# A two-layer decoder trunk on one core: FoX queries and keys by halves, w_out in landing order, memory norm emitted earlier

## The chip, the core and the metric

The kernel runs on one NeuronCore of one Trainium2 chip. The metric is the device time of one execution in microseconds, and the runs are compared by their median. The engines are TensorE (PE, matrix products; PEld is its weight load), VectorE (DVE), ScalarE (ACT), GpSimd (POOL) and SyncE (SP), which here issues all DMAs. Each engine works through its own queue in order, and semaphores hold an instruction until its data are there.

## The reference

Two identical layers on x of 256 tokens by 1024 features, in float32. Each layer does four things, all before an RMSNorm and added to x:

```python
x = x + 0.5 * swiglu(rms_norm(x, ffn1_norm[l]), ...)
x = x + hybrid_mixer(rms_norm(x, mix_norm[l]), w_in[l], ..., w_out[l])
x = x + memory_cross_attention(rms_norm(x, cross_norm[l]), rms_norm(mem, mem_norm[l]), ...)
x = x + 0.5 * swiglu(rms_norm(x, ffn2_norm[l]), ...)
```

The change is in the mixer. One projection `z = h @ w_in` gives HGRN2's q, f, i, g (four heads of 128) and FoX's q, k, v and a forget logit (eight heads of 64). HGRN2 is a gated scan over the tokens, with an output norm and gate. FoX is causal softmax attention whose scores carry the accumulated log forget gates as a bias. Their outputs are joined and multiplied by `w_out`. The cross attention reads 256 memory tokens; its keys are made from the normalized memory.

## The kernel before

**Products.** Every float32 factor is cut into a rounded high part and the rest, and a product is three matmuls, high x high, high x low and low x high (`mm3`, L379; the low x low part is left out). Weights come by DMA as 1 MB loads into three `raw` buffers (`fetch`, L126). ScalarE casts the high part (L149) and VectorE subtracts it (L150); both go into pools of seven buffers, `whi` and `wlo`, of `SLOT` columns. `plan` lists every load of the program in order, `take` (L156) hands out the next one, splits one load ahead and fetches two more beyond that.

There are three kinds of product. `xstat` (L388) has the tokens stationary and up to 512 weight columns moving: the result has tokens on the partitions. `wstat` (L420) has a 128x128 block of weights stationary and 256 tokens moving: the result is feature-major; it took two loads, 512 columns wide, and ran through all eight row blocks of a column block before the next. `rows_to_residual` (L470) contracts over the rows of w_out or another output matrix: the first two blocks for all four accumulators, then for each accumulator the last six (`TAIL`), so that the first half of the tokens is done early and its norm can start.

**Order.** The emission order is worked out at build time by a small planner (`drive`, L341). Tasks are Python generators that yield the TensorE time that they used, a latency, or an `Event`; a spawned task runs as soon as the planner's clock has reached it, before the main line. The clock is that of the plan and not the chip's: constants such as `LAT_M` say how long a task is to leave its results alone. A scheduler then places the emitted instructions on the engines' queues, with the buffers of each pool handed out as they come free. One pool, `s4`, has 19 buffers of 4 KB a partition for nearly all activations.

**The mixer** (L794). `xstat_first` makes v and the output gate. Then come, main line first: `wstat` for the forget gates `fg` and the keys `kk`; `wstat` for q; the spawn of `hgrn` (L572), which runs seven levels of a blocked scan, each with small matmuls (`al`, L589) and VectorE updates of `qf` and `kk` (L610, L612); the spawn of `memory_task` (L874), which loads and normalizes the memory, waits `LAT_M`, and transposes it to `mf`; a 260-wide `xstat` with FoX's v for heads 4 to 7 and the forget logits; the spawn of `fox_gates` (L676); `wstat` for FoX q, then k, 512 wide; a 260-wide `xstat` for the rest of v. Then two FoX lanes are spawned (`fox_lane`, L741), each with two pairs of heads one after the other: a pair's score operands are stacked (`fox_stack`, L719), scores, softmax, transposes and the product with v follow. The main line meanwhile makes the cross keys `kc` from `mf` (L858 to L865) and then contracts `w_out`, whose first four row blocks are HGRN2's (`ev_h`) and whose last four are FoX's pairs 0 to 3 (`ev_p`).

The lanes and the order before:

```python
fox_lane((lane, lane + 2), fq, fk, fv, L_, R_, oT, cmask, oh, ev_g, ev_p)
```

Of the kernel before, what the change touches and what calls it, by code (L numbers as in the profile page):

```python
# [12 lines left out]
AF = mybir.ActivationFunctionType  # L13
# [7 lines left out]
D = 1024  # L21
# [4 lines left out]
EPS = 1e-6  # L26
NEG = -1.0e30
FCH = [(c, min(512, DFF - c)) for c in range(0, DFF, 512)]
SLOT = 1040
N_S4, N_W = 19, 7  # L30
TAIL = 6
HP = 100
# [1 line left out]
LAT_NORM, LAT_X = 5.5, 6.5  # L34
LAT_LVL, LAT_AX, LAT_HN = 3.0, 1.0, 3.5
LAT_FS, LAT_FT, LAT_CQ, LAT_CS, LAT_CT = 6.0, 2.5, 2.6, 5.6, 3.0
LAT_Q, LAT_G1, LAT_G2, LAT_M = 5.0, 9.0, 2.0, 18.0
LAT_HT = 2.4
LAT_FK = 5.0

# [5 lines left out]
def hymba_kernel(  # L46
# [43 lines left out]
    def add_cols(w, l, c0, cw):  # L90
        for k0 in range(0, KT, 4):
            plan.append((kview(w, l, c0, cw, k0, 4), 4, cw))

    def add_rows(w, l, nkt):
        for k0 in range(0, nkt, 2):
            plan.append((kview(w, l, 0, D, k0, 2), 2, D))
# [7 lines left out]
    for l in range(DEPTH):  # L104
        add_ffn(ffn1_g, ffn1_u, ffn1_d, l)
        for o in (OFF_I, OFF_G, OFF_F, OFF_Q):
            add_cols(w_in, l, o, 512)
        add_cols(w_in, l, OFF_FV + 260, 260)
        add_cols(w_in, l, OFF_FQ, 512)
        add_cols(w_in, l, OFF_FK, 512)  # L110
        add_cols(w_in, l, OFF_FV, 260)
        add_cols(c_wk, l, 0, 512)
        add_cols(c_wk, l, 512, 512)
        add_rows(w_out, l, KT)
        for w in (c_wv, c_wq):
            for c0 in (0, 512):
                add_cols(w, l, c0, 512)
        add_rows(c_wo, l, KT)
        add_ffn(ffn2_g, ffn2_u, ffn2_d, l)
# [16 lines left out]
    def split(i):  # L136
        while len(pieces) <= min(i, len(plan) - 1):
            j = len(pieces)
            fetch(j + LA_D - 1)
            _, nk, cw = plan[j]  # L140
            r = raws[j]
            n = max(1, SLOT // cw)
            res = []
            for k0 in range(0, nk, n):
                kk = min(n, nk - k0)
                sl = r[:, k0 * cw:(k0 + kk) * cw]
                hi = wp.tile([P, SLOT], F32R, name=nm("whi"), tag="whi")
                lo = wp.tile([P, SLOT], F32R, name=nm("wlo"), tag="wlo")
                nc.scalar.copy(out=hi[:, :kk * cw], in_=sl)  # L149
                nc.vector.tensor_tensor(out=lo[:, :kk * cw], in0=sl,  # L150
                                        in1=hi[:, :kk * cw].bitcast(F32), op=ALU.subtract)
                for k in range(kk):
                    res.append((hi[:, k * cw:(k + 1) * cw], lo[:, k * cw:(k + 1) * cw]))
            pieces.append(res)
# [264 lines left out]

    def wstat(f, use, cw=512):  # L420

        pc = take() + take()
        for b in range(cw // 256):
            ps = acc()
            for j in range(2):
                c = (2 * b + j) * P
                for kt in range(KT):
                    mm3(ps[:, j * S:(j + 1) * S], pc[kt][0][:, c:c + P], pc[kt][1][:, c:c + P],
                        f.hi(kt), f.lo(kt), kt == 0, kt == KT - 1)
                    yield T256  # L430
            use(b, ps)
# [306 lines left out]
            nc.gpsimd.tensor_copy(out=ks[oth, 1, sub, :], in_=R_[oth])  # L738
        return qs, ks

    def fox_lane(pairs, fq, fk, fv, L_, R_, oT, cmask, oh, ready, done):  # L741
        yield ready
        for pr in pairs:
            qs, ks = fox_stack(pr, fq, fk, L_, R_, oh)
            yield (LAT_FK,)
            prs = []
            for sub in range(2):
                ps = smp("fs")
                for t, o, n in SEGS:
                    for j in range(2):  # L750
                        nc.tensor.matmul(ps[:, o:o + n], lhsT=qs[:, j, sub, t * P:(t + 1) * P], rhs=ks[:, j, sub, 0:n],
                                         start=j == 0, stop=j == 1)
                yield 0.44
                pr_ = pp()
                prs.append(pr_)
                mx = small(2, "fmx")
                for t, o, n in SEGS:
                    nc.vector.tensor_tensor_reduce(out=pr_[:, o:o + n], in0=ps[:, o:o + n], in1=cmask[:, S - n:S],
                                                   scale=1.0, scalar=-3.0e38, op0=ALU.add, op1=ALU.max,
                                                   accum_out=mx[:, t:t + 1])  # L760
                nmx = small(2, "fnm")
                nc.vector.tensor_scalar(out=nmx, in0=mx, scalar1=-1.0, scalar2=None, op0=ALU.mult)
                softmax(pr_, nmx, 1.0, [(t, pr_[:, o:o + n], pr_[:, o:o + n]) for t, o, n in SEGS])
            yield (LAT_FS,)
            pTs = []
            for sub in range(2):
                pt = smp("fpt")
                for j in range(3):
                    nc.tensor.transpose(pt[:, j * P:(j + 1) * P], prs[sub][:, j * P:(j + 1) * P], ident)
                yield 3 * T1  # L770
                pT = sm.tile([P, 512], F32, name=nm("ppT"), tag="ppT", bufs=4)
                nc.scalar.copy(out=pT[:, 0:3 * P], in_=pt[:, 0:3 * P])
                pTs.append(pT)
            yield (LAT_FT,)
            pv = smp("fpv")
            for sub in range(2):
                h = 2 * pr + sub
                b0 = sub * 64
                vs = slice(h * 64, (h + 1) * 64)
                pT = pTs[sub]  # L780
                o = pv[b0:b0 + 64]
                nc.tensor.matmul(o[:, 0:P], lhsT=fv[:, 0, vs], rhs=pT[:, 0:P], start=True, stop=True)
                nc.tensor.matmul(o[:, P:S], lhsT=fv[:, 0, vs], rhs=pT[:, P:2 * P], start=True, stop=False)
                nc.tensor.matmul(o[:, P:S], lhsT=fv[:, 1, vs], rhs=pT[:, 2 * P:3 * P], start=False, stop=True)
                yield 0.64
            put_split(oT.h[1][:, pr, :], oT.l[1][:, pr, :], pv[:, 0:S])
            done[pr].fire(1.6)

    def feat_major(f, func, scale, dst):
        def use(b, ps):  # L790
            nc.scalar.activation(dst[:, 2 * b:2 * b + 2, :], ps.rearrange("p (k t) -> p k t", k=2), func, scale=scale)
        return wstat(f, use)

    def mixer(cur, l, consts, nxt_w):  # L794
        masks, tri, cmask, sel, oh = consts
# [13 lines left out]
        for t in range(NT):  # L809
            nc.scalar.activation(gw[:, t, :], pg[t], AF.Silu)  # L810
            gv = gw[:, t, :].rearrange("p (h e) -> p h e", h=4)
            nc.vector.tensor_tensor(out=gv, in0=gv, in1=onw.unsqueeze(1).to_broadcast([P, 4, P]), op=ALU.mult)

        fg = s4([P, 4, S], F32, "fg")
        kk = s4([P, 4, S], F32, "kk")
# [12 lines left out]
        q = s4([P, 4, S], F32, "hq")  # L828
        yield from feat_major(f, AF.Silu, 1.0, q)
        oT = Feat("oT")  # L830
        ev_h, ev_q, ev_m, ev_g = Event(), Event(), Event(), Event()
        ev_q.fire(LAT_Q)
        spawn(hgrn(q, fg, kk, v, gw, oT, masks, ev_q, ev_h))
        mf = Feat("mf")
        spawn(memory_task(l, wmem, mf, ev_m))
        fv = s4([P, NT, 512], F32, "fv")
        zb = small(16, "zb", bufs=2).rearrange("p (t h) -> p t h", t=NT)
        ps = []
        yield from xstat(f, 260, ps)
        for t in range(NT):  # L840
            nc.vector.tensor_tensor(out=zb[:, t, :], in0=ps[t][:, 252:260], in1=fb, op=ALU.add)
            nc.scalar.copy(out=fv[:, t, 260:512], in_=ps[t][:, 0:252])
        L_ = sm.tile([P, S], F32, name=nm("L"), tag="L", bufs=1)
        R_ = sm.tile([P, S], F32, name=nm("R"), tag="R", bufs=1)
        spawn(fox_gates(zb, L_, R_, tri, sel, ev_g))
        fq = s4([P, 4, S], F32, "fq")
        yield from feat_major(f, AF.Copy, 0.125, fq)
        fk = s4([P, 4, S], F32, "fk")
        yield from feat_major(f, AF.Copy, 1.0, fk)
        ps = []  # L850
        yield from xstat(f, 260, ps)
        for t in range(NT):
            nc.scalar.copy(out=fv[:, t, 0:260], in_=ps[t][:, 0:260])
        oT.alloc(1)
        ev_p = [Event() for _ in range(4)]
        for lane in range(2):
            spawn(fox_lane((lane, lane + 2), fq, fk, fv, L_, R_, oT, cmask, oh, ev_g, ev_p))
        kc = [[s4([P, 4, S], F32R, "kc") for _ in range(2)] for _ in range(2)]  # L858
        yield ev_m
        for c in range(2):  # L860
# [3 lines left out]

            yield from wstat(mf, use)  # L865
        nxt = Next(nxt_w, lat=LAT_X)

        def act(kt, t):
            return oT.hi(kt, t), oT.lo(kt, t)

        yield from rows_to_residual(act, KT, 1.0, TAIL, nxt, lambda kt: ev_h if kt < 4 else ev_p[kt - 4])
        return nxt, kc, mf

    def memory_task(l, wn, mf, ev):  # L874
        mf.alloc(0)
        mf.alloc(1)
        ms = []
        for t in range(NT):
            mt = s4([P, D], F32, "mem")
# [8 lines left out]
            apply_norm(mt, rs)  # L888
            ms.append(mt)
        yield (LAT_M,)  # L890
        for t in range(NT):
            for b in range(2):
                to_feat(ms[t], t, mf, b)
# [124 lines left out]
```

## Time and profile before

| | us |
|---|---|
| median of 3 runs | 1253.11 (1252.86 to 1255.58) |
| profiled execution | 1254.4 |
| its span, first to last instruction | 1252.6 |
| mean granted TensorE clock | 0.997 of full |

A row of busy time by stage gives the length of the stretch, the busy microseconds of each engine with its number of instructions, the granted clock, the share of the DMA engines and the bytes moved. A row of waits gives the engine and line that stood, what ended it, the total, how often, and the longest. A row of a group of instructions gives line, engine, operation, output and inputs, shapes and count, then busy us and mean ns, then the engine's idle time before them. Matmuls are pipelined: the next starts before the modelled end of the one before.

### The profile page before, as it was taken

What the parts mean: (1) busy time and instruction counts of PE and PEld (TensorE: products, weight loads), DVE (VectorE), ACT (ScalarE), POOL (GpSimd) and SP (SyncE); (2) the same over time, 40 slices, a digit from 0 to 9 for tenths busy, and PEclk for the clock granted to TensorE, in tenths of its full rate; (3) what the DMA queues carried; (4) which work ended last, traced back from release to release, by engine and by line L of the source; (5) the groups of instructions that cost most, each with busy time, mean ns of one, the idle gap of its engine ahead of it and who ended that gap; (6) DMA issues with size and microseconds to landing.
All of it is one profiled execution on the core that took longest, in us unless ns stands there. A gap on an engine that the chain in (4) does not pass through costs nothing.

```text
span 1252.6 us, 21298 instructions
## 1 busy us (share of the span) xinstructions
PE 1225.4 (98%) x8969; PEld 1118.6 (89%) x8969; DVE 758.6 (61%) x1108; ACT 628.4 (50%) x935; POOL 38.2 (3%) x52
## 2 busy tenths in 40 slices
PE   6999999999999999999999999999999999999997
PEld 4999988989889889998889998889998898999986
DVE  6654646597875674555474555476786766545643
ACT  5544434567854464454354454265585645534531
POOL 0000000002000000000000000000020000000000
PEclk9999999999999999999999999999999999999999
DMA  7654754654444264556474556465443633555650
GB/s 268 221 195 136 249 195 151 212 158 157 146 172 170 101 233 154 203 174 219 145 240 147 202 180 219 140 219 186 138 156 113 234 119 136 170 200 168 236 169 34
DMA packets 100752, 221.26 MB, mean 177 GB/s; under 512 B 4136, under 2 KB 16688, under 8 KB 100656
## 3 DMA queue, kind: packets, MB, share of 16 engines
q1 hardware_dynamic: 100656, 219.90, 51.6%
q8 instruction: 70, 1.15, 0.4%
q14 instruction: 26, 0.21, 0.1%
HBM read 218.84 MB, written 1.05 MB: 176 GB/s over the span
## 4 chain that ended last, share of the span: by engine, by line
PE 90%; ACT 4%; DVE 3%; DMA 1%; issue 1%; POOL 0%; SPq 0%; POOLq 0%; DVEq 0%; ACTq 0%
PE acc L380 28%; PE acc L381 28%; PE acc L382 28%; PE pt L301 1%; ACT whi L149 1%; DVE wlo L150 1%; ACT pp L713 1%; ACT fqs L729 1%; DMA mem<-in_mem_dram 1%; PE al L589 1%; DMA raw<-in_ffn_w_gate_dram 1%; ACT fks L731 1%; ACT fks L730 0%; POOL mrs L282 0%; PE cpo L381 0%
## 5 line engine op out<-in xcount | busy, mean ns | idle before, releaser
L150 DVE TENSOR_TENSOR wlo<-raw,whi 128x1024 fp32r<-128x1024 f32 x400 | 479.3, 1224 | 323.6 <-ACT whi L149 322.2
L149 ACT CAST whi<-raw 128x1024 fp32r<-128x1024 f32 x400 | 406.4, 1047 | 337.1 <-PE acc L382 183.9
L380 PE MATMUL acc<-xfh,whi 128*128 128x256 f32 x1536 | 434.9, 283 | 0.0
L381 PE MATMUL acc<-xfl,whi 128*128 128x256 f32 x1536 | 431.9, 281 | 0.0
L382 PE MATMUL acc<-xfh,wlo 128*128 128x256 f32 x1536 | 430.0, 280 | 1.9 <-DVE wlo L150 1.9
L382 PEld LDWEIGHTS acc<-xfh,wlo 128*128 128x128 f32 x1536 | 290.4, 189 | 2.2 <-DVE wlo L150 2.2
L381 PEld LDWEIGHTS acc<-xfl,whi 128*128 128x128 f32 x1536 | 290.9, 189 | 0.4
L380 PEld LDWEIGHTS acc<-xfh,whi 128*128 128x128 f32 x1536 | 289.2, 188 | 0.9
L380 PE MATMUL acc<-whi,hth 128*128 128x512 f32 x352 | 138.6, 394 | 0.0
L381 PE MATMUL acc<-wlo,hth 128*128 128x512 f32 x352 | 138.5, 393 | 0.0
L382 PE MATMUL acc<-whi,htl 128*128 128x512 f32 x352 | 138.1, 392 | 0.0
L380 PE MATMUL acc<-whi,xfh 128*128 128x512 f32 (+1 forms) x256 | 95.2, 373 | 1.8 <-ACT xfh L307 1.8
L381 PE MATMUL acc<-wlo,xfh 128*128 128x512 f32 (+1 forms) x256 | 94.5, 369 | 0.0
L382 PE MATMUL acc<-whi,xfl 128*128 128x512 f32 (+1 forms) x256 | 94.2, 368 | 0.0
L382 PEld LDWEIGHTS acc<-whi,htl 128*128 128x128 f32 x352 | 66.2, 188 | 15.1
L380 PEld LDWEIGHTS acc<-whi,hth 128*128 128x128 f32 x352 | 66.1, 188 | 14.9
L381 PEld LDWEIGHTS acc<-wlo,hth 128*128 128x128 f32 x352 | 66.1, 188 | 14.7
L380 PEld LDWEIGHTS acc<-whi,xfh 128*128 128x128 f32 x256 | 48.6, 190 | 10.3 <-ACT xfh L307 2.2
L382 PEld LDWEIGHTS acc<-whi,xfl 128*128 128x128 f32 x256 | 48.6, 190 | 8.9 <-DVE xfl L308 0.6
L288 ACT ACTIVATE jk<-xs 128x512 f32<-128x512 f32 x36 | 21.7, 603 | 68.4 <-DVE xs L482 66.6
L381 PEld LDWEIGHTS acc<-wlo,xfh 128*128 128x128 f32 x256 | 48.7, 190 | 7.9
L307 ACT CAST hth<-sil 128x512 fp32r<-128x512 f32 x36 | 22.3, 621 | 62.2 <-DVE sil L556 62.2
(228 smaller groups left out, 1340.3 us busy)
## 6 DMA issues: line engine op xcount, KB each, us to landing
raw<-in_ffn_w_down_dram SPq DMA_DIRECT2D x44, 1024.0 KB, 4.9
raw<-in_ffn_w_up_dram SPq DMA_DIRECT2D x40, 1024.0 KB, 5.3
raw<-in_ffn_w_gate_dram SPq DMA_DIRECT2D x38, 1024.0 KB, 5.2
raw<-in_w_in_dram SPq DMA_DIRECT2D x24, 1024.0 KB, 5.3
raw<-in_cross_wk_dram SPq DMA_DIRECT2D x8, 1024.0 KB, 5.1
raw<-in_w_out_dram SPq DMA_DIRECT2D x8, 1024.0 KB, 5.0
raw<-in_cross_wv_dram SPq DMA_DIRECT2D x8, 1024.0 KB, 5.2
raw<-in_cross_wq_dram SPq DMA_DIRECT2D x8, 1024.0 KB, 5.6
```

The source lines that it names most:

```text
L149: nc.scalar.copy(out=hi[:, :kk * cw], in_=sl)
L150: nc.vector.tensor_tensor(out=lo[:, :kk * cw], in0=sl, in1=hi[:, :kk * cw].bitcast(F32), op=ALU.subtract)
L288: nc.scalar.activation(dst, half(src, j), AF.Square, scale=1.0 / 32.0, accum_out=ss[:, j:j + 1])
L301: nc.tensor.transpose(pt[:, j * P:(j + 1) * P], hn[:, kt * P:(kt + 1) * P], ident)
L307: nc.scalar.copy(out=hi, in_=src)
L380: nc.tensor.matmul(ps, lhsT=lh, rhs=rh, start=start, stop=False)
L381: nc.tensor.matmul(ps, lhsT=lh, rhs=rl, start=False, stop=False)
L382: nc.tensor.matmul(ps, lhsT=ll, rhs=rh, start=False, stop=stop)
L589: nc.tensor.matmul(ps[s0:s0 + hb, c0:c0 + hb], lhsT=k[:, h, a:a + hb], rhs=rhs[:, h, a + step:a + step + hb], start=True, stop=True)
L713: nc.scalar.activation(dst, src, AF.Exp, bias=nmx[:, t:t + 1], scale=scale, accum_out=sms[:, t:t + 1])
L729: nc.scalar.copy(out=qs[own, :, sub, :], in_=qv.unsqueeze(1).to_broadcast([64, 2, S]))
L731: nc.scalar.copy(out=ks[oth, 0, sub, :], in_=kv)
```

## The change

FoX's q and k are loaded and computed by halves of 256 columns: first the halves of heads 4 to 7 (q, then k), then those of heads 0 to 3. One load holds all eight row blocks of a half, so `wstat` takes one load where it has eight blocks. The two lanes are spawned after the first two halves and run pairs 2 and 3 first, then 0 and 1; a lane's stack follows an event for its half of k, its product with v one for its half of v. The v columns are cut 264 and 256 instead of 260 and 260, and `SLOT` grows by 16 columns. `w_out` is loaded and contracted with the row blocks of pairs 2 and 3 ahead of those of 0 and 1. `memory_task` is spawned ahead of the forget gates; its feature buffers are taken after its delay, and the delay is 34 instead of 18. FoX's output buffers are taken when the first pair is done. The number of casts in a split is rounded down to a power of two.

```diff
-SLOT = 1040
+SLOT = 1056
-LAT_Q, LAT_G1, LAT_G2, LAT_M = 5.0, 9.0, 2.0, 18.0
+LAT_Q, LAT_G1, LAT_G2, LAT_M = 5.0, 9.0, 2.0, 34.0
+    def add_half(w, l, c0):
+        plan.append((kview(w, l, c0, 256, 0, KT), KT, 256))
-        add_cols(w_in, l, OFF_FV + 260, 260)
-        add_cols(w_in, l, OFF_FQ, 512)
-        add_cols(w_in, l, OFF_FK, 512)
-        add_cols(w_in, l, OFF_FV, 260)
+        add_cols(w_in, l, OFF_FV + 256, 264)
+        for c0 in (256, 0):
+            add_half(w_in, l, OFF_FQ + c0)
+            add_half(w_in, l, OFF_FK + c0)
+        add_cols(w_in, l, OFF_FV, 256)
...
-        add_rows(w_out, l, KT)
+        for k0 in (0, 2, 6, 4):
+            plan.append((kview(w_out, l, 0, D, k0, 2), 2, D))
...
-            n = max(1, SLOT // cw)
+            n = 1 << (SLOT // cw).bit_length() - 1
...
     def wstat(f, use, cw=512):
-        pc = take() + take()
+        pc = take()
+        if len(pc) < KT:
+            pc = pc + take()
...
-    def fox_lane(pairs, fq, fk, fv, L_, R_, oT, cmask, oh, ready, done):
+    def fox_lane(pairs, fq, fk, fv, L_, R_, oT, cmask, oh, ready, ev_k, ev_v, done):
         yield ready
         for pr in pairs:
+            yield ev_k[pr // 2]
             qs, ks = fox_stack(pr, fq, fk, L_, R_, oh)
...
             yield (LAT_FT,)
+            yield ev_v[pr // 2]
             pv = smp("fpv")
...
+            if 1 not in oT.h:
+                oT.alloc(1)
...
-    def feat_major(f, func, scale, dst):
+    def feat_major(f, func, scale, dst, b0=0, cw=512):
         def use(b, ps):
+            b += b0
...
-        return wstat(f, use)
+        return wstat(f, use, cw)
...
     def mixer(cur, l, consts, nxt_w):
...
+        ev_h, ev_q, ev_m, ev_g = Event(), Event(), Event(), Event()
+        mf = Feat("mf")
+        spawn(memory_task(l, wmem, mf, ev_m))
         fg = s4([P, 4, S], F32, "fg")
...
-        mf = Feat("mf")
-        spawn(memory_task(l, wmem, mf, ev_m))
...
-        yield from feat_major(f, AF.Copy, 0.125, fq)
         fk = s4([P, 4, S], F32, "fk")
-        yield from feat_major(f, AF.Copy, 1.0, fk)
+        ev_k, ev_v = [Event(), Event()], [Event(), Event()]
+        ev_p = [Event() for _ in range(4)]
+        ev_v[1].fire()
+        for hf in (1, 0):
+            yield from feat_major(f, AF.Copy, 0.125, fq, hf, 256)
+            yield from feat_major(f, AF.Copy, 1.0, fk, hf, 256)
+            ev_k[hf].fire()
+            if hf == 1:
+                for lane in range(2):
+                    spawn(fox_lane((lane + 2, lane), fq, fk, fv, L_, R_, oT, cmask, oh, ev_g, ev_k, ev_v, ev_p))
         ps = []
-        yield from xstat(f, 260, ps)
+        yield from xstat(f, 256, ps)
...
-        oT.alloc(1)
-        ev_p = [Event() for _ in range(4)]
-        for lane in range(2):
-            spawn(fox_lane((lane, lane + 2), fq, fk, fv, L_, R_, oT, cmask, oh, ev_g, ev_p))
+        ev_v[0].fire()
...
+        order = (0, 1, 2, 3, 6, 7, 4, 5)
         def act(kt, t):
+            kt = order[kt]
             return oT.hi(kt, t), oT.lo(kt, t)
...
-        yield from rows_to_residual(act, KT, 1.0, TAIL, nxt, lambda kt: ev_h if kt < 4 else ev_p[kt - 4])
+        def need(kt):
+            kt = order[kt]
+            return ev_h if kt < 4 else ev_p[kt - 4]
+
+        yield from rows_to_residual(act, KT, 1.0, TAIL, nxt, need)
...
     def memory_task(l, wn, mf, ev):
-        mf.alloc(0)
-        mf.alloc(1)
         ms = []
...
         yield (LAT_M,)
+        mf.alloc(0)
+        mf.alloc(1)
```

More of the change, by code (lines that the diff above doesn't have):

```diff
@@ L830, in mixer @@
         oT = Feat("oT")
-        ev_h, ev_q, ev_m, ev_g = Event(), Event(), Event(), Event()
         ev_q.fire(LAT_Q)
         spawn(hgrn(q, fg, kk, v, gw, oT, masks, ev_q, ev_h))
-        mf = Feat("mf")
-        spawn(memory_task(l, wmem, mf, ev_m))
         fv = s4([P, NT, 512], F32, "fv")
@@ L838, in mixer @@
         ps = []
-        yield from xstat(f, 260, ps)
+        yield from xstat(f, 264, ps)
         for t in range(NT):
-            nc.vector.tensor_tensor(out=zb[:, t, :], in0=ps[t][:, 252:260], in1=fb, op=ALU.add)
-            nc.scalar.copy(out=fv[:, t, 260:512], in_=ps[t][:, 0:252])
+            nc.vector.tensor_tensor(out=zb[:, t, :], in0=ps[t][:, 256:264], in1=fb, op=ALU.add)
+            nc.scalar.copy(out=fv[:, t, 256:512], in_=ps[t][:, 0:256])
         L_ = sm.tile([P, S], F32, name=nm("L"), tag="L", bufs=1)
@@ L846, in mixer @@
         fq = s4([P, 4, S], F32, "fq")
-        yield from feat_major(f, AF.Copy, 0.125, fq)
         fk = s4([P, 4, S], F32, "fk")
-        yield from feat_major(f, AF.Copy, 1.0, fk)
+        ev_k, ev_v = [Event(), Event()], [Event(), Event()]
[8 more added lines that the diff above has]
+                    spawn(fox_lane((lane + 2, lane), fq, fk, fv, L_, R_, oT, cmask, oh, ev_g, ev_k, ev_v, ev_p))
         ps = []
-        yield from xstat(f, 260, ps)
+        yield from xstat(f, 256, ps)
         for t in range(NT):
-            nc.scalar.copy(out=fv[:, t, 0:260], in_=ps[t][:, 0:260])
-        oT.alloc(1)
-        ev_p = [Event() for _ in range(4)]
-        for lane in range(2):
-            spawn(fox_lane((lane, lane + 2), fq, fk, fv, L_, R_, oT, cmask, oh, ev_g, ev_p))
+            nc.scalar.copy(out=fv[:, t, 0:256], in_=ps[t][:, 0:256])
+        ev_v[0].fire()
         kc = [[s4([P, 4, S], F32R, "kc") for _ in range(2)] for _ in range(2)]
```

## The prediction

> **What bounds the kernel now.** I read the page first, then who TensorE waited for in the mixer of each layer, then busy time and granted clock by stage.
>
> ```profile
> PE 1225.4 (98%) x8969; PEld 1118.6 (89%) x8969; DVE 758.6 (61%) x1108; ACT 628.4 (50%) x935; POOL 38.2 (3%) x52
> ```
>
> TensorE is busy for 98% of the span and the others for 61% at most, so only time in which TensorE stands, or runs at a lower clock, can be won. Its waits from 250 to 346 us (layer 0) and from 860 to 962 us (layer 1), columns: total us, times, longest:
>
> ```profile
> PE acc L380 <- DVE kc L308: 1.4, 1, 1.4
> PE acc L382 <- DVE wlo L150: 1.0, 1, 1.0
> PE al L589 <- DVE kk L612: 0.6, 1, 0.6
> PE al L589 <- DVE qf L580: 0.4, 1, 0.4
> PE fpv L782 <- ACT ppT L772: 0.4, 1, 0.4
> PE fs L751 <- DVE fks L734: 0.3, 2, 0.2
> ...
> PE acc L380 <- DVE kc L308: 1.5, 1, 1.5
> PE acc L382 <- DVE wlo L150: 1.0, 1, 1.0
> PE al L589 <- DVE kk L612: 0.6, 1, 0.6
> PE fpv L782 <- ACT ppT L772: 0.4, 1, 0.4
> PE fs L751 <- DVE fks L734: 0.3, 2, 0.2
> ```
>
> That is 4.1 us in 7 waits and 3.8 us in 6. Two groups: at the start of the HGRN2 scan (al, wlo: 2.0 and 1.6 us) and in the FoX rounds and behind them (fs, fpv, kc: 2.1 and 2.2 us). Nearly all end on VectorE. Next, layer 0 by stage (v and gate projection; forget gates; q; the 260-wide product with the start of the scan; FoX q, k and rest of v; cross keys with FoX; start of w_out), then two stretches of layer 1, and the costliest matmul group:
>
> ```profile
> 205.00:228.00 23.00, 22.99 (x105) 18.52 (x104) 18.23 (x21) 13.69 (x19) 2.37 (x2) 1.00 0.83 273
> 228.00:240.00 12.00, 12.00 (x102) 11.91 (x101) 5.25 (x10) 6.73 (x9) 0.00 (x0) 1.00 0.19 50
> 240.00:252.00 12.00, 12.00 (x104) 12.00 (x103) 6.49 (x10) 6.94 (x10) 0.00 (x0) 1.00 0.93 330
> 252.00:262.00 10.00, 8.99 (x190) 8.49 (x188) 8.87 (x20) 7.72 (x15) 2.39 (x2) 1.00 0.56 184
> 262.00:303.00 41.00, 40.00 (x592) 38.60 (x593) 33.20 (x58) 23.64 (x51) 5.05 (x8) 1.00 0.47 156
> 303.00:337.00 34.00, 32.91 (x270) 31.24 (x268) 30.07 (x101) 30.35 (x75) 2.01 (x3) 1.00 0.26 94
> ...
> 875.00:880.00 5.00, 3.66 (x76) 3.27 (x77) 4.45 (x6) 1.02 (x1) 0.00 (x0) 0.73 0.39 99
> 880.00:885.00 5.00, 5.00 (x97) 4.68 (x95) 3.47 (x11) 2.31 (x4) 0.00 (x0) 0.93 0.41 119
> ```
>
> ```profile
> L382 PE MATMUL acc<-xfh,wlo 128*128 128x256 f32 x1536 | 430.0, 280 | 1.9 <-DVE wlo L150 1.9
> ```
>
> Columns of the stages: length, busy us of PE, PEld, DVE, ACT, POOL, granted clock, DMA share, GB/s. Two things besides the waits are lost. A wait is counted from the modelled end of a matmul, 280 ns after its start, but in the q stage 104 matmuls start in 12.00 us, one per 0.12 us; so each of the 13 waits costs 0.16 us more, 2.1 us together. And in layer 1 the waits at the scan's start are followed by a granted clock of 0.73 and 0.93 over 5 us each: 5 x 0.27 + 5 x 0.07 = 1.7 us. Layer 0, with the same waits, kept 1.00. **Everything that the mixer's waits cost is 7.9 + 2.1 + 1.7 = 11.7 us**, the ceiling of this change.
>
> The Trainium skill, "TensorE: Matmul & The Clock Gate", section "HAM oscillation — how this bites in real kernels", gives as the rule that no idle gap of TensorE may exceed about 3.4 us. The waits above are 1.5 us at most and the clock fell all the same, so the trace does not agree that shorter gaps are free. By the rule the drop has another cause and may stay; the sum below would then be 1.7 us less of a gain, 1247.1.
>
> **The change part by part.** *Memory norm earlier.* Its instructions, both layers together (min/median/max ns):
>
> ```profile
> L288 ACT ACTIVATE mj<-mem x8: 580/587/602, 250.7 to 868.1; 128x512 f32<-128x512 f32 x8
> L288 ACT ACTIVATION_READ_ACCUMULATOR mj<-mem x8: 186/187/189, 251.2 to 868.6; 128x1 f32 x8
> L291 DVE TENSOR_TENSOR mem<-mem,wn x8: 682/686/693, 251.5 to 869.5; 128x512 f32<-128x512 f32 x8
> L295 DVE TENSOR_SCALAR mem<-mem,mrs x8: 478/484/486, 255.3 to 872.2; 128x512 f32<-128x512 f32 x8
> L880 SPq DMA_DIRECT2D mem<-in_mem_dram x4: 444/484/618, 241.7 to 856.1; - x4
> ...
>   DVE mem L295: 1.8, 4
> ```
>
> Per layer this is 4 x 0.686 + 4 x 0.484 = 4.7 us of VectorE plus 0.9 us in which its queue stands for the power on GpSimd (the last row), and 4 x 0.77 = 3.1 us of ScalarE. It sits at 251 to 260 us, in the stage where VectorE is busy 8.87 of 10 us and TensorE first stands. TensorE's lateness there is 2.0 us; taking 5.6 us out of VectorE's queue covers it, and with it the clock drop. The work goes to the forget-gate stage, busy 5.25 (VectorE) and 6.73 (ScalarE) of 12 us, where 5.6 and 3.1 fit. Its two DMAs (0.48 us of SP each) are now issued ahead of the second 264-wide load instead of ahead of the first FoX key load; that leaves a stage with a DMA share of 0.93 for one with 0.19. If ScalarE reaches the squares before memory has landed, the gate sigmoids and later weight casts queue behind them; the cover is the slack of these stages, which show no wait of TensorE. Without that cover it costs the 3.1 us of squares per layer. I take 0. Late next would be the memory transposes, wanted only by the cross keys at 303 us; they move little, since their delay grows from 18 to 34 planner units while their start comes forward by two 512-wide passes. Worth: 2.0 + 1.6 us of waits, 5 restarts (0.8) and 1.7 of clock, 6.1 us.
>
> *Halves, and FoX heads 4 to 7 first.* Same matmuls, casts and bytes: 260 + 260 columns become 264 + 256, and a 1 MB weight load takes 8 row blocks of 256 columns instead of 4 of 512. Its landing has no row; nearest:
>
> ```profile
> raw<-in_w_in_dram SPq DMA_DIRECT2D x24, 1024.0 KB, 5.3
> raw<-in_ffn_w_gate_dram SPq DMA_DIRECT2D x12, 512.0 KB, 3.8
> ```
>
> It lies between 5.3 us and twice the 3.8 us of a 512 KB load that already has 256-wide rows, 7.6. I take 5.3, since the bytes set the larger loads. A half pass is 48 matmuls at 0.12, 5.8 us; four loads late by 1.8 us each would be 7.2 us, inside the two passes (11.5 us) by which three raw buffers run ahead. Cost 0. The new events are the planner's: on the chip an instruction still waits for its data and its buffer alone.
>
> What moves is VectorE and ScalarE work of two of four FoX pairs. All four in layer 0, by tile, for PE, PEld, DVE, ACT (score stacks; probabilities, where the 2.21 belongs to the gates; transposed probabilities):
>
> ```profile
> sum 141.00, PE 4.74 PEld 4.11 DVE 6.13 ACT 4.98; mean PE 1.18 PEld 1.03 DVE 1.53 ACT 1.24
> sum 141.00, PE 4.74 PEld 4.11 DVE 3.35 ACT 6.47 POOL 5.03; mean PE 1.18 PEld 1.03 DVE 0.84 ACT 1.62 POOL 1.26
> 262.00:303.00 41.00, 0.00 (x0) 0.00 (x0) 2.21 (x5) 0.37 (x1) 1.00 0.47 156
> sum 141.00, PE 3.36 PEld 2.77 DVE 11.49 ACT 7.94; mean PE 0.84 PEld 0.69 DVE 2.87 ACT 1.99
> sum 141.00, PE 4.20 PEld 3.47 DVE 0.00 ACT 3.42; mean PE 1.05 PEld 0.87 DVE 0.00 ACT 0.85
> ```
>
> VectorE 6.1 + 3.4 + 9.3 = 18.8, ScalarE 5.0 + 6.5 + 7.6 + 3.4 = 22.5; half is 9.4 and 11.2. They leave the key stage (30.07 and 30.35 of 34 become 20.7 and 19.1) for the one before (33.20 and 23.64 of 41 become 42.6 and 34.8). The 5.6 us that the memory norm frees just ahead let the weight subtractions standing at 262 us be done by then, so VectorE's 42.6 becomes about 39 to 41 of 41: full, no more. In the key stage both engines then have a third free, so the wait of w_out's fourth accumulator for the last key eviction (1.4 and 1.5) goes. Both rounds start two half passes and a v pass sooner, 3 x 5.8 = 17 us, and w_out asks for pairs 0 and 1 last; it hides w_out's reorder too, costed at 0. Worth with fs and fpv: 4.3 us and 8 restarts (1.3), 5.6 us.
>
> *What comes back.* VectorE is full from 262 to 303 us with the scan, whose matmuls stand in TensorE's in-order queue. Low bound: nothing, because the stage today is at 33.20 of 41 and loses nothing that the waits show but what it inherited. High bound: the 252 to 262 stage, which at 8.87 of 10 loses 1.0 us in 10, 4.1 us a layer. I take 2.0 a layer, halfway: the FoX waits recurring in the first round (fs, fpv and three restarts, 1.2) and one more of the scan.
>
> **Sum.** 11.7 - 4.0 = 7.7 us. Profiled execution 1254.4 us (span 1252.6, 1.8 around it), so 1246.7; the median of the runs, 1253.1, is 1.3 lower: **1245.4 us**. With nothing or 4.1 a layer coming back: 1241.4 to 1249.6, the forecast's own range.
>
> **Rivals.** *The wait only moves* (no change): VectorE full for 41 us loses at the rate of the 252 to 262 stage, 4.1 us and four restarts (0.6) a layer, and the clock drops once as today: 9.4 + 1.7 = 11.1 of 11.7 is given back, 1252.5. For it: 39 to 41 of 41; against it: weight subtractions are emitted a pass ahead, so it is FoX that slips, and FoX has 17 us. Chance 0.18.
>
> *The scan starves TensorE* (slower): scan levels, weight subtractions and the first FoX round share VectorE's queue, and each scan matmul holds everything behind it on TensorE. At the rate of the 875 to 880 stretch, 1.34 us lost of 5 with VectorE at 4.45 of 5, for half of the 41 us: 5.5 us a layer, and 1.7 of clock in both: 14.4 us, so 1253.1 - 11.7 + 14.4 = 1255.8. It decides from 5.9 us a layer upward without the clock, 4.2 with it. Against it: that stretch was caused by the norm that leaves. Chance 0.18.
>
> *FoX doesn't start early.* When the first two pairs want four of the pool's 19 large buffers, 17 are held: normalized x 4, v, gate, k, scaled q, scan matrix, decay products, FoX v, q and k, memory 4. The second pair waits for a release, and if both end up behind the scan only the memory part pays: 1253.1 - 6.1 = 1247.0. Against it: the first pair's two fit. Chance 0.12.
>
> **Numbers.** Forecast 0.52. A change under 0.2% (2.5 us) can't be told from none. Faster: 0.52 + 0.12, 0.64; the same: the first rival, 0.18; slower: the second, 0.18. Range 1241 (the ceiling) to 1256, which leaves out about half of the slower rival.
>
> **What would show it.** Right: no wait of al for qf or kk and none of acc for wlo right after the first scan matmuls; granted clock 1.00 there in both layers; memory squares before 242 us; first exp before 300 us; no wait for kc at w_out; VectorE over 90% between the 264-wide product and the keys, below 70% in the keys. Wrong: TensorE waits for kk, fks or wlo of over 2 us a layer in that stage, a new clock drop, casts standing for the memory DMA, or FoX stacks after the scan's last level.

## The result and the profile after

| | before | after |
|---|---|---|
| median of the runs | 1253.11 us (1252.86 to 1255.58) | 1258.61 us (1257.09 to 1260.3) |
| profiled execution, its span | 1254.4, 1252.6 us | 1258.61, 1256.8 us |

The change makes the kernel slower, by a ratio of 1.0043 (95% interval 1.003 to 1.0056), 5.5 us at the medians. 1245.4 was predicted, with a range from 1241 to 1256.

The page after, engines and granted clock in 40 slices:

```profile
PE 1232.8 (98%) x8969; PEld 1124.5 (89%) x8969; DVE 759.0 (60%) x1108; ACT 630.7 (50%) x935; POOL 36.7 (3%) x52
...
PEclk9999999999999999999999999999899999999999
```

The instruction counts are those of before on every engine, but TensorE is busy for 7.4 us more, and one slice, around 900 us, has a lower clock. What TensorE waited for from 250 to 346 us, and then from 860 to 965 us:

```profile
PE fs L759 <- ACT fks L738: 1.3, 1, 1.3
PE al L596 <- issue: 0.5, 1, 0.5
PE fpt L777 <- DVE pp L724: 0.3, 1, 0.3
PE hot L673 <- DVE oh L667: 0.3, 1, 0.3
PE fs L759 <- DVE fks L741: 0.2, 1, 0.2
...
PE fs L759 <- ACT fks L738: 1.4, 1, 1.4
PE acc L386 <- issue: 0.6, 1, 0.6
PE fpt L777 <- DVE pp L724: 0.3, 1, 0.3
PE hot L673 <- DVE oh L667: 0.3, 1, 0.3
```

The waits at the start of the scan (`wlo`, `kk`, `qf`) and the one for the last key (`kc`) are gone. In their place stands one large wait per layer that is new: the scores of a FoX pair (`fs`) wait for ScalarE's copies into the pair's stack (`fks`). The other rows are of 0.6 us at most, and "issue" is standing for which the profile shows no cause. All together it is 2.6 us in each layer, less than before (4.1 and 3.8). The stages after, with the same columns as before, then 900 to 910 us:

```profile
228.00:240.00 12.00, 12.00 (x103) 11.97 (x102) 10.26 (x19) 9.48 (x17) 2.00 (x3) 1.00 0.43 159
...
252.00:262.00 10.00, 10.00 (x228) 9.68 (x229) 9.76 (x20) 6.89 (x10) 0.00 (x0) 1.00 0.73 213
262.00:303.00 41.00, 38.42 (x565) 35.38 (x550) 34.45 (x89) 30.77 (x76) 5.66 (x7) 1.00 0.38 130
303.00:337.00 34.00, 34.00 (x289) 32.59 (x289) 22.33 (x61) 21.00 (x49) 1.36 (x3) 1.00 0.26 94
900.00:905.00 5.00, 3.52 (x18) 2.72 (x18) 4.18 (x20) 4.84 (x10) 0.38 (x1) 0.80 0.59 208
905.00:910.00 5.00, 5.00 (x32) 4.88 (x31) 3.65 (x19) 4.07 (x14) 0.00 (x0) 0.52 0.01 3
```

The key stage no longer has a gap (34.00 of 34 instead of 32.91), but the stage ahead of it now has a larger one (38.42 of 41 instead of 40.00). VectorE is not full there, 34.45 of 41. And at 900 to 910 us the clock fell to 0.80 and 0.52: 5 x 0.20 + 5 x 0.48 = 3.4 us of full-speed time lost, where before had lost 1.7 us at 875 us.

Why the stack was late shows in ScalarE's instructions one by one (start, duration, instruction):

```profile
281.86 1.65 ACT L634 COPY A<-Ac 32x256 f32<-32x256 f32 x4
283.52 0.74 ACT L627 COPY A<-al 32x256 f32<-32x256 f32 x2
284.29 0.62 ACT L736 CAST fqs<-fq 64x512 fp32r<-64x512 f32 x1
284.81 0.40 ACT L737 CAST fks<-fk 64x256 fp32r<-64x256 f32 x1
285.24 0.40 ACT L738 CAST fks<-fk 64x256 fp32r<-64x256 f32 x1
```

The scan's six copies of `A` are ahead of the second pair's stack in ScalarE's in-order queue, and the first scores of that pair need three casts behind them (`fqs`, `fks`, `fks`). The last of these ends at 285.64, and the scores start at 285.69 after 1.28 us of standing.

One more difference lies outside the mixer, where the change moves nothing. Ninety microseconds of the first FFN (only 256-wide matmuls, all with the weights stationary), before and then after; columns: length, TensorE busy with its number of matmuls, granted clock, DMA share, GB/s:

```profile
45.00:135.00 90.00, 90.00 (x767) 1.00 0.52 175
```

```profile
45.00:135.00 90.00, 90.00 (x761) 1.00 0.51 172
```

At the same clock, and with no wait in either, six matmuls fewer fit into 90 us. From the start times of all such matmuls (4992 in the program), the mean from one start to the next is 117.8 ns before and 118.7 ns after: 4992 x 0.85 ns = 4.2 us.

### The profile page after: what moved, and what is told of

Same layout as the page of the kernel before. It is cut to its first block, busy times and chain, and to the rows that moved or that the text cites. A ratio compares the mean times of both kernels' runs of the same rounds, so it can differ in the third digit from the quotient of the medians.

```text
span 1256.8 us, 21287 instructions
## 1 busy us (share of the span) xinstructions
PE 1232.8 (98%) x8969; PEld 1124.5 (89%) x8969; DVE 759.0 (60%) x1108; ACT 630.7 (50%) x935; POOL 36.7 (3%) x52
## 4 chain that ended last, share of the span: by engine, by line
PE 95%; ACT 2%; DVE 1%; DMA 1%; issue 0%; SPq 0%; POOLq 0%; DVEq 0%; ACTq 0%
PE acc L385 30%; PE acc L387 29%; PE acc L386 29%; PE pt L306 1%; DMA raw<-in_ffn_w_gate_dram 1%; PE al L596 1%; PE fs L759 1%; PE cpo L386 0%; PE cpo L387 0%; PE cs L387 0%; PE cs L386 0%; PE cs L385 0%; PE cpo L385 0%; PE fpt L777 0%; PE fpv L791 0%
## 5 line engine op out<-in xcount | busy, mean ns | idle before, releaser
L385 PE MATMUL acc<-whi,xfh 128*128 128x512 f32 (+2 forms) x256 | 94.8, 372 | 1.6 <-ACT xfh L312 1.6
L386 PE MATMUL acc<-wlo,xfh 128*128 128x512 f32 (+2 forms) x256 | 94.3, 368 | 0.0
L387 PE MATMUL acc<-whi,xfl 128*128 128x512 f32 (+2 forms) x256 | 94.0, 367 | 0.0
```

The lines of the kernel that those rows point to most:

```text
L385: nc.tensor.matmul(ps, lhsT=lh, rhs=rh, start=start, stop=False)
L386: nc.tensor.matmul(ps, lhsT=lh, rhs=rl, start=False, stop=False)
L387: nc.tensor.matmul(ps, lhsT=ll, rhs=rh, start=False, stop=stop)
```

## The experiments

"Weights, activations" gives the bytes modulo 128 at which the stationary weights (`whi`, `wlo`) and the moving activations (`xfh`, `xfl`) start in a partition, worked out from the buffers' addresses in the built program. With 1040 columns a weight buffer is 4160 bytes long, so that every other one starts 64 bytes further; with 1056 it is 4224 bytes, 33 x 128, and all start alike. "Clock" is the mean over the runs of the granted clock, and "lost" is (1 - clock) x time. The kernel before, over the 52 runs that it had beside these, has a clock of 0.9984 and loses 2.0 us. The clock of a run is recorded to 0.001, which is 1.3 us. A part of "lost" costs no time: in the profiled execution of every kernel the clock is at half for the last 2 to 5 us, 1.0 to 2.6 us lost, when TensorE has no matmul left. For before, with the columns of the stages:

```profile
1249.40:1252.60 3.20, 0.00 (x0) 0.00 (x0) 0.00 (x0) 0.00 (x0) 0.00 (x0) 0.50 0.40 152
```

So only differences of "lost" between kernels are read below.

| run | weights, activations | median us (range) | ratio to before, 95% | ns per 256-wide matmul | clock, lost us |
|---|---|---|---|---|---|
| before | 32 and 96, 32 | 1253.0 (1251.0 to 1255.5) | 1 | 117.8 | 0.9984, 2.0 |
| after | 32, 32 | 1258.61 (1257.09 to 1260.3) | 1.0043 (1.003 to 1.0056) | 118.7 | 0.9962, 4.8 |
| e1: before, 1056 columns | 32, 32 | 1255.85 (1255.05 to 1257.97) | 1.0022 (1.0013 to 1.0031) | 118.7 | 0.9986, 1.7 |
| e2: after, 1040 columns | 32 and 96, 32 | 1257.85 (1257.06 to 1259.8) | 1.0038 (1.0024 to 1.0051) | 117.8 | 0.9960, 5.0 |
| e3: after, weights moved | 96, 32 | 1236.72 (1233.13 to 1240.56) | 0.9868 (0.985 to 0.9886) | 113.4 | 0.9956, 5.4 |
| e4: after, activations moved | 32, 96 | 1235.56 (1235.08 to 1237.97) | 0.9862 (0.9849 to 0.9876) | 113.4 | 0.9968, 4.0 |
| e5: after, both moved | 96, 96 | 1260.03 (1258.87 to 1261.12) | 1.0056 (1.004 to 1.0071) | 118.7 | 0.9960, 5.0 |
| e6: e1 + memory norm | 32, 32 | 1254.64 (1253.89 to 1255.73) | 1.0017 (1.0008 to 1.0026) | 118.7 | 0.9984, 2.1 |
| e7: after without memory norm | 32, 32 | 1260.35 (1259.35 to 1261.42) | 1.0058 (1.0044 to 1.0073) | 118.7 | 0.9962, 4.8 |
| e8: e1, activations moved | 32, 96 | 1237.16 (1235.44 to 1238.19) | 0.9872 (0.9856 to 0.9887) | 113.4 | 0.9985, 1.9 |
| e9: after, scores later | 32, 32 | 1255.08 (1253.94 to 1255.9) | 1.0014 (1.0006 to 1.0023) | 118.7 | 0.9976, 3.0 |
| e10: e4, scores later | 32, 96 | 1234.68 (1232.86 to 1235.61) | 0.9854 (0.984 to 0.9867) | 113.4 | 0.9970, 3.7 |
| e11: e8 + memory norm | 32, 96 | 1233.49 (1232.6 to 1235.65) | 0.9848 (0.9834 to 0.9861) | 113.4 | 0.9976, 3.0 |
| e12: as e11, activations at 64 | 32, 64 | 1262.07 (1261.68 to 1262.69) | 1.0067 (1.005 to 1.0084) | 119.2 | 0.9988, 1.6 |

### Is it the size of the weight buffers? (e1, e2)

e1 is the kernel before with that one number of the change, e2 the changed kernel without it:

```diff
-SLOT = 1040
+SLOT = 1056
```

> The kernel before with SLOT 1056 in place of 1040, nothing else. The weight pieces whi and wlo then start every 4224 bytes instead of every 4160: in the kernel before 32 and 96 bytes past a multiple of 128 in turn, now 32 all of them, as in the changed kernel. Theory A (the buffers' place sets the pitch of the 256-wide matmuls): their start-to-start goes from 117.8 to about 118.7 ns in every stage; 4992 of them by 0.85 ns is 4.2 us, so 1257.3. Theory B (the new order of the mixer costs it): the order is the old one, so 1253.1.

> The changed kernel with SLOT 1040: pieces start 32 and 96 bytes past a multiple of 128 in turn again, and each 264-wide load is cast in two pieces of 528 columns instead of one of 1056. Theory A: pitch back at 117.8 ns, 1258.6 - 4.2 = 1254.4; what is left against 1253.1 is the worth of the new order. Theory B: 1258.6.

e1 runs the order of before, with its waits, and takes 2.8 us more, about half of the whole loss. Its rate in the FFN is that of the changed kernel, and e2's is that of before; e1, then e2:

```profile
45.00:135.00 90.00, 90.00 (x760) 1.00 0.51 172
```

```profile
45.00:135.00 90.00, 90.00 (x766) 1.00 0.52 178
```

So the rate goes with the buffer size and not with the halves. The 4.2 us of matmuls come out as 2.8 in the runs; by the means of the runs without what each lost to the clock, as 3.2 (1254.27 against 1251.03). e2 has the rate that the first theory expected, but not its 1254.4 us: it still takes 4.8 us more than before: its 264-wide split takes two casts instead of one, and it lost 5.0 us to the clock, so the order of the work, or its second cast, has a price of its own; e7 below has no second cast and shows that it is the order.

### Size, or place? (e3, e4, e5)

The sizes stay at 1056. A small pool of 64 bytes a partition ahead of the weights' or of the activations' pool moves all that lies behind it; e4 has `pads` only, ahead of the activations, e5 `padw` only, ahead of the weights and so of all that follows, e3 both (which brings the activations back to 32):

```diff
+    padw = ctx.enter_context(tc.tile_pool(name="padw", bufs=1))
+    pads = ctx.enter_context(tc.tile_pool(name="pads", bufs=1))
+    ps_ = pads.tile([P, 16], F32, name="ps_")
+    nc.gpsimd.memset(ps_, 0.0)
```

> The changed kernel with 64 unused bytes ahead of the weight pieces and 64 ahead of the activations: pieces all at 96 past a multiple of 128, activations at 32 as before. Theory A: 116.6 ns, the pitch that the matmuls of the kernel before show whose weights lie at 96: 2.1 ns by 4992 less, 1248.2. Theory B: 1258.6.

> The changed kernel with 64 unused bytes ahead of the activations alone: pieces at 32, activations at 96. If only the distance between weights and moving activations counts (A, relative): 116.6 ns as with the pieces moved, 1248.2. If the place of the weights alone counts (A, absolute): 118.7 ns, 1258.6. Theory B: 1258.6.

> The changed kernel with 64 unused bytes ahead of the weight pieces, so that pieces and activations both lie at 96 past a multiple of 128. If the pitch goes by the distance between the two (equal: slow): 118.7 ns and 1258.6. If one of the two at 96 is what made the last two kernels fast: 113.4 ns and about 1236.

With weights and activations 64 bytes apart, whichever of them is moved, the changed kernel takes 1236.7 and 1235.6 us, 22 and 23 us less; with both moved by the same 64 bytes it takes 1260.0 again. The same 90 us of e4 and of e5:

```profile
45.00:135.00 90.00, 90.00 (x797) 1.00 0.55 190
```

```profile
45.00:135.00 90.00, 90.00 (x761) 1.00 0.51 171
```

797 matmuls instead of 761, and TensorE waits for nothing in either. So the place of the one operand relative to the other changes the rate. e3 and e4 are faster than the 116.6 ns and 1248.2 us expected: 116.6 is what matmuls with weights at 96 take in the kernel before, where weights at 32 are mixed in, so there the operands' own distance isn't all that counts. The 512-wide matmuls, where the activations are stationary, keep their 231 ns in all of these. How the two operands hinder each other inside the chip no run shows.

### Which half of the change costs? (e6, e7)

Both with 1056 columns: e6 is the kernel before with the memory norm moved, e7 the changed kernel with the memory norm where it was and a delay of 18. These lines of the change are in e6 and not in e7:

```diff
+        mf = Feat("mf")
+        spawn(memory_task(l, wmem, mf, ev_m))
...
-LAT_Q, LAT_G1, LAT_G2, LAT_M = 5.0, 9.0, 2.0, 18.0
+LAT_Q, LAT_G1, LAT_G2, LAT_M = 5.0, 9.0, 2.0, 34.0
```

> The kernel before with SLOT 1056 (1255.85 by itself) and the memory norm's move alone: spawn ahead of the gates, feature buffers after the delay, delay 34. Theory M (the move does what was forecast, FoX's early start costs): al and wlo waits at the scan's start gone, 3.6 us of waits and 5 restarts, 1251.5. Theory N (the move itself costs, by work in the gate stage): 1257 or more.

> The changed kernel with the memory norm back in its old place (spawn after q, feature buffers first, delay 18); halves, FoX order and w_out order stay. Theory M: the wait of fs for ScalarE's stack (1.3 and 1.4 us) and one or two drops of the clock (1.7 us each) stay and the waits at the scan's start are back: 1260 to 1263. Theory N: 1253 to 1255.

Against e1, the memory norm alone gives 1.2 us by the medians and 0.6 by the ratios (whose intervals overlap, so it can't be told from nothing by these runs); e6 came between what its two theories expected. FoX by halves alone costs 4.5, and by the runs' means 3.1 of it are clock (4.8 lost against 1.7); its waits are 4.3 and 3.2 us in the two layers, against 3.3 and 3.7 in e1. e6's waits in layer 0:

```profile
PE acc L380 <- DVE kc L308: 0.8, 1, 0.8
PE fs L751 <- DVE oTl L308: 0.5, 1, 0.5
PE fs L751 <- ACT fks L731: 0.5, 1, 0.5
PE fs L751 <- DVE fks L734: 0.2, 1, 0.2
```

The waits at the scan's start are gone, as predicted (`wlo` 0.6 and `kk` 0.6 in e1's layer 0), and `kc` fell from 1.4 to 0.8; but with TensorE earlier, FoX's scores now stand for their stack and for VectorE, 0.5 and 0.5 us. Of 2.3 us won in that layer (`fpv`'s 0.4 is gone too) 1.0 comes back two stages later. Over both layers e6 stands 2.6 us less than e1 (4.4 against 7.0), more than the runs gained; where the rest went is not shown.

### Is it ScalarE's queue? (e9, e10)

The scores of a pair are placed later behind its stack, in the changed kernel (e9) and in e4 (e10):

```diff
-LAT_FK = 5.0
+LAT_FK = 9.0
```

> The changed kernel with one number different: the scores of a FoX pair are placed 9 planner units behind its stack instead of 5, so TensorE reaches them later in its order. Theory (ScalarE's queue makes the first score stacks late, TensorE stands 1.3 and 1.4 us for them, and the half-clock stretch of layer 1 follows from that standing): the waits of fs for the ACT copies of fks fall to under 0.4 us together, no stretch near 903 us at half clock, mixers of 141.2 to 142 us, median 1253 to 1255.5. Rival (the clock stretches belong to early FoX work as such, not to the wait): waits gone, clock stretch stays, 1256 to 1257. Rival (the wait only moves on to the transposed probabilities or to w_out): 1258 to 1260.

> The same number, 9 for 5, in the changed kernel whose activations lie 64 bytes apart from its weights (1235.6 us). Theory: the waits of fs (3.3 us in all there) and the half-clock stretches (5.1 us lost in its profiled execution) mostly go, 1230 to 1233. Rival (the wait moves on): 1235 to 1237. In both the 256-wide matmuls start one per 113.4 ns.

e9 wins 3.5 of the changed kernel's 5.5 us back. Its waits in layer 1, and the clock from 900 to 915 us:

```profile
PE ho L653 <- ACT AX L643: 1.4, 1, 1.4
PE fs L759 <- DVE fqs L739: 1.3, 1, 1.3
PE fpt L777 <- DVE AX L667: 0.6, 1, 0.6
PE acc L387 <- issue: 0.4, 1, 0.4
PE hot L673 <- DVE oh L667: 0.2, 1, 0.2
```

```profile
900.00:905.00 5.00, 5.00 (x50) 4.77 (x48) 3.10 (x5) 2.82 (x6) 0.99 (x2) 1.00 0.64 210
905.00:910.00 5.00, 3.54 (x27) 3.12 (x26) 4.82 (x25) 4.70 (x8) 0.22 (x1) 1.00 0.02 5
910.00:915.00 5.00, 3.64 (x33) 3.44 (x32) 3.48 (x16) 4.99 (x24) 0.00 (x0) 1.00 0.22 52
```

The theory held by its time and fell by half of its mechanism. The wait for ScalarE's stack copies is gone, but another `fs` wait (on VectorE, for the same stack) and one of the scan's `ho` took its place: TensorE stands for 3.9 us in this layer, 1.3 more than in the changed kernel. What went, in the profiled execution, is the stretch at half clock, though gaps of 1.3 and 1.4 us are still there between 905 and 915 us. Over all its runs e9 loses 3.0 us to the clock and the changed kernel 4.8, so up to 1.8 of the 3.5 us are clock. For the rest the traces offer FoX's small matmuls, whose starts are closer together in e9 (the 48 of `fpv` take 3.5 us instead of 4.4 in each layer); that it is they was not tried. In e10 the same edit gives 0.9 us, which its interval does not tell from e4's; its time lies between the two ranges expected.

### Does the move pay with the faster matmuls? (e8, e11), and what of other distances? (e12)

e8 is e1 and e11 is e6, each with the 64 bytes ahead of the activations; e12 is e11 with 32 bytes:

```diff
-    ps_ = pads.tile([P, 16], F32, name="ps_")
+    ps_ = pads.tile([P, 8], F32, name="ps_")
```

> The kernel before with SLOT 1056 and 64 unused bytes ahead of the activations: old order, fast place of the buffers. If the new order costs the same there (2.75 us, as between the changed kernel and the one before with SLOT 1056): 1235.6 - 2.75 = 1232.8. If a faster TensorE gains by the new order (VectorE and ScalarE are tighter): over 1236.

> The kernel before with buffers of 1056 columns, the memory norm moved as in the change, and the activations 64 bytes apart from the weights; no halves. Theory (the two effects add: layout from e8, memory move worth 1.2 from e6 against e1): 1235.5 to 1236.5. Rival (with TensorE faster by 4% VectorE's lateness in the scan weighs more and the move is worth 3 or more): 1232 to 1234.5. Rival (what it gains at the scan's start comes back in the key stage in full): 1237 to 1238.

> The kernel of the eleventh run with the activations moved up by 32 bytes instead of 64, so that weights lie at 32 and activations at 64 of each 128 bytes; same instructions in the same order. Theory (what counts is whether the two operands lie in the same half of 128 bytes, or 64 bytes apart, and 32 apart shares a half for part of it): between the two, some 116 ns a matmul and 1243 to 1248 us. Rival (any distance other than zero is fast): 113.4 ns, 1233 to 1235. Rival (only the distance of 64 is fast): 118.7 ns, 1253 to 1256.

The 64 bytes give 18.7 us to the order of before (e1 to e8) and 23 to the changed one (after to e4). 5.3 ns less for each of 4992 matmuls would be 26 us. In an FFN, 864 of them, it comes out whole: 188.4 us becomes 183.9. In the mixer of the old order it does not: from the first projection's first matmul to the last of w_out, 156.6 us in both layers become 156.2 and 155.7, though 576 matmuls there would give 3.1 us. TensorE's waits grow instead, from 3.3 and 3.7 us to 4.9 and 4.4, nearly all of them for VectorE. There the memory norm is worth more: e11 takes 3.7 us less than e8 by the medians, 3.0 by the ratios, whose intervals overlap by a little; of the three cases expected, the one of 3 us or more came. e11's waits in layer 1:

```profile
PE acc L383 <- DVE kc L311: 1.0, 1, 1.0
PE fs L754 <- ACT fks L734: 0.8, 1, 0.8
PE acc L385 <- issue: 0.7, 1, 0.7
PE fs L754 <- DVE oTl L311: 0.7, 1, 0.7
PE fs L754 <- DVE fks L737: 0.2, 1, 0.2
```

e11 is the fastest kernel of this study, 1233.49 us, 19.6 less than before; it has no halves at all. e10, which has everything, is 1.2 us behind it, with intervals that overlap.

In e12, with the operands 32 bytes apart, none of the three expected cases came: the 256-wide matmuls are slower than at the same place (119.2 ns), and the 512-wide ones are slower too, 233.3 ns from start to start instead of 231.0. Ninety microseconds of e12:

```profile
45.00:135.00 90.00, 90.00 (x756) 1.00 0.51 172
```

Since in e12 alone an operand lies at a multiple of 64 bytes, and as the 512-wide ones changed only there, the place itself may count beside the distance; one run does not separate the two.

## Why the prediction was wrong, point by point

The forecast had 0 for the buffers' place (which it doesn't name), 6.1 us won by the memory norm, and 5.6 - 4.0 = 1.6 us won by the halves with what comes back. The runs that change one of them at a time show +2.8 (e1), -1.2 (e6 against e1) and +4.5 us (e7 against e1). These add up to +6.1, and the change measured +5.5.

**"Same matmuls, casts and bytes ... Cost 0".** This step failed first. The matmuls are the same in number and shape, but 16 more columns of `SLOT` put all their weights at the place of the activations, and each of 4992 matmuls became 0.85 ns slower, most of them in stages that the change doesn't touch. The missing term is +4.2 us by the matmuls, +2.8 in the runs (e1). The trace of before held a hint that was not read: by the start times and the addresses, matmuls with weights at 96 started every 116.6 ns, those with weights at 32 every 118.9.

**"What comes back: VectorE is full from 262 to 303 us", 2.0 us a layer.** The amount of standing was about right, 2.6 us a layer, the engine was wrong, and the price was too low. VectorE had 6.5 us free in that stage. The late one was ScalarE, busy 30.77 of 41, far from full: six small copies ahead of three casts in an in-order queue were enough. The share of busy time was taken for the measure of lateness; what counted was who stands ahead of whom at one moment. With FoX's scores placed 4 units later (e9) the changed order is 0.8 us faster than e1, and level with the memory norm alone (e6: 0.4 slower by the medians, 0.4 faster by the ratios): halves, as such, show neither a gain nor a cost.

**"Clock, 1.7 us" to be won.** The drop at 875 us in the profiled execution of before was read as part of every execution. Over 52 runs before has a mean clock of 0.9984, and 37 of them have 0.999; the 14 at 0.997 or less are on average 2.0 us longer (1254.5 against 1252.5). The profiled one was of those. So less could be won, and it was lost instead: all kernels in which FoX starts early and its scores come 5 units after the stack (after, e2 to e5, e7) lose 4.0 to 5.4 us to the clock; before, e1, e6, e8 and e12 lose 1.6 to 2.1, and e11 3.0. By the means of the runs, the 5.8 us between before and after are 2.7 of clock, 3.2 of the buffers' place and about -0.2 for everything else, the waits among it, if each us lost costs one. It may cost less: those 14 runs of before lose 2.9 us more than the 37 and are 2.0 longer. By that the clock is 1.9 and the rest 0.7; either rest is too small to be told from nothing.

**"Memory norm: 6.1 us".** The mechanism was right: squares now start at 229.7 us, the waits for `qf`, `kk` and `wlo` are gone, and the clock at 870 to 890 us is 1.00. ScalarE did stand for the memory's load, 1.1 us in two waits, with the gates' work queued behind it. The size was wrong: 1.2 us (e6 against e1). A part of the standing came back as the FoX scores' own wait (1.0 us a layer), and the 1.7 us of clock are not lost in most executions of before; the rest is not accounted for. The cover named for ScalarE's wait, the slack of the gate stages, held: 12.00 of 12 us busy on TensorE in both.

**"Halves: 5.6 us".** `kc` is gone at w_out, the first exp starts at 290.0 us and VectorE is at 66% in the key stage, all as foretold; the key stage gained its 1.1 us. The stage ahead lost 1.6 us in TensorE's busy time. The load of 256 columns with eight row blocks brought no wait, so cost 0 was right for that part.

**The slower rival** had the right side and nearly the time, 1255.8, but for the wrong reason: its price came from VectorE at 4.45 of 5 us. Its term for the clock, a drop in each layer, is the part that the profile bore out, 3.4 us there too, but at 900 us alone; that TensorE stood more, the waits don't show (7.9 us before, some 5 after). **FoX doesn't start early** fell: the first scores started at 281.7 us, before at 307.8.

**The rule from the Trainium skill**, "TensorE: Matmul & The Clock Gate", section "HAM oscillation — how this bites in real kernels" (no idle gap over about 3.4 us), was set aside because the clock fell after gaps of 1.5 us at most. The runs bear this out: after a gap of 1.4 us the clock fell to half in the changed kernel, and after gaps of 1.3 and 1.4 us it did not in e9's profile. The Trainium skill, same page, section "What's actually happening", has the clock set by how busy TensorE was in a window of about 3.4 us that runs on freely and does not start anew with a kernel. The clock records of the traces agree: inside the kernels the granted clock is 1.00 or 0.50, and the stretches are whole multiples of 3.41 us (in the changed kernel 259, then 2 at half clock, then 101). Cut along this grid, and leaving out the half clock at each execution's end, all 10 falls in the 14 traces came right after one window in which TensorE was busy for 49 to 59%. Of the full-clock windows as thin as that, 10 were followed by half clock and 9 were not, and none of the fuller ones was. The window ahead of the fall and the fall in the changed kernel, then the window with the gap of 1.3 us in e9:

```profile
899.56:902.97 3.41, 1.95 (x13) 1.39 (x12) 2.63 (x7) 3.27 (x9) 0.76 (x2) 1.00 0.85 289
902.97:909.79 6.82, 6.80 (x36) 6.31 (x37) 5.43 (x31) 6.07 (x16) 0.00 (x0) 0.50 0.04 13
...
904.23:907.64 3.41, 1.95 (x16) 1.66 (x15) 3.29 (x12) 2.58 (x6) 0.93 (x2) 1.00 0.01 2
```

Both windows have 1.95 us busy of 3.41, and only the first was followed by half clock. So a short gap is a risk, by how much else is thin beside it and by where the grid falls in that execution. What tells the 10 from the 9 the traces don't show.

## What to carry to other kernels

Where a buffer's size changes, work out where the operands then lie, and compare the start-to-start time of matmuls in an untouched stage before any other row; a matmul loop that waits for nothing can still be 4 to 5% off. Ask of a moved task which instructions will be queued just ahead of it on each in-order engine, not how busy the engine is in the stage. And read the clock over many runs before it goes into a sum: one profiled execution either has a drop or hasn't.

## What the runs showed of the hardware

- A 256-wide float32 matmul with its weights stationary starts every 113.4 ns where weights and activations start 64 bytes apart modulo 128, every 118.7 ns where they start at the same place (32 or 96), and every 119.2 ns at 32 and 64. With half of the weights apart and half not it is 117.8, closer to the slow rate than to the middle: 116.6 for those apart and 118.9 for the others.
- A 512-wide matmul with the activations stationary takes 230.8 to 231.7 ns at all of these places but 32 and 64, where it takes 233.3.
- TensorE's granted clock falls to half for 3.41 or 6.83 us after a window of 3.41 us in which it was busy for 49 to 59% (10 of 19 such windows in 14 traces), also where the longest gap was 1.4 us. It does so in some executions and not in others of the same kernel: before's runs have mean clocks from 0.996 to 0.999.
